# A 3x3 convolution with bfloat16 matmuls: row blocks with a shared middle tap, or every row computed directly

## The chip, the cores and the metric

The kernel runs on one core of a Trainium2 chip. The metric is device time in microseconds (us) of one execution. "PE" is the matrix engine (TensorE), "DVE" the vector engine, "ACT" the scalar engine, "POOL" GpSimd, and "SP" the engine whose queue issues most of the stores.

## The reference

Sixteen images of 64 channels and 64 x 64 pixels are convolved with 128 filters of 3 x 3, with a border of zeros. About nine in ten weights are zero, at random places; neither kernel makes use of that.

```python
batch, c_in, h, w, c_out, k = 16, 64, 64, 64, 128, 3
x_pad = np.pad(x, ((0, 0), (0, 0), (1, 1), (1, 1)))
# for every b, co, ci, kh, kw:
output[b, co] += weight[co, ci, kh, kw] * x_pad[b, ci, kh:kh+h, kw:kw+w]
```

Inputs and output are float32. The input has 16.8 MB, the output 33.6 MB.

## The kernel before

**Placing.** Two images form a pair: the 64 channels of one lie on partitions 0 to 63, those of the other on partitions 64 to 127. There are eight pairs (`NP`), each a resident bfloat16 tile `xs[p]`. Line 63 loads the weights through SP's queue, line 64 the first 9 rows of pair 0 as float32 (`x_head`) through ACT's queue; ACT casts them on line 79. The other rows of pair 0 come in two transfers (lines 65 and 66, up to row 25 and from row 26), and pairs 1 to 7 in one each (line 70). All of these are issued by POOL's queue and cast on the way. While loads are under way, PE runs seven matmuls on zeros (line 77).

**Weights.** DVE casts the weights into `w_bf` (line 101), one group for each kernel row: G0, G1 and G2. `transposed` (lines 91 to 96) turns a group with three matmuls against an identity and copies the result to `wT`. `tap` gives the 64 x 128 weights of a kernel row and column for the upper or lower half of the partitions.

**A product.** `product` (lines 119 to 140) takes two PSUM tiles, one for each image of the pair, and adds up terms. A term is a source, a weight group, a first row and a step between rows. Each term costs three matmuls (kernel columns) for each image, issued in turns: image 0 on the upper 64 rows of the array, image 1 on the lower 64. One matmul covers 8 rows of 64 pixels, 512 columns; at the left and right border 8 x 63, and where a kernel row falls off the image 7 rows.

**Two ways to get 16 output rows.** `direct` (lines 142 to 147) computes 8 rows from three terms, 9 matmuls for each image, and ACT copies one image from PSUM to the output tile `o`, DVE the other. `twos` (lines 149 to 168) computes 16 rows at once. With rows x[r] and x[r+1] of a two-row step, the outputs are

- even row r: G1 (x[r] + x[r+1]) + (G2 - G1) x[r+1] + G0 x[r-1]
- odd row r+1: G1 (x[r] + x[r+1]) + (G0 - G1) x[r] + G2 x[r+2]

so the product of G1 with the sum serves both. POOL adds the row couples into `s` (line 152), PE multiplies by G1 (3 matmuls for each image, 8 rows of sums), ACT copies the result to `pc` (line 159), PE does the even rows and then the odd rows with two terms each (6 matmuls for each image), and DVE adds `pc` to each (line 166). That is 15 matmuls for each image and 16 rows, where `direct` needs 18. The differences G21 = G2 - G1 and G01 = G0 - G1 are made on line 110 by DVE and turned by `transposed`; `differences` is called after the first `direct` group of pair 0.

**Order.** The schedule is written by hand: each engine works in program order. Pairs follow each other, and in a pair four blocks of 16 rows. `BLOCKS` says which blocks are done directly (D): the first of pair 0 and the last of pair 7; the other 30 are T. Output tiles rotate through 7 buffers, PSUM tiles through 8, `s` through 3, `pc` through 4. The stores of a pair, 2 MB for each image, are issued by SP when the pair is done (line 195). Those of pair 7 go out in pieces: rows 0 to 31 and 32 to 47 (line 192, SP), and the last two groups of 8 rows each by themselves (line 183 on SP, line 186 on ACT's queue).

Of the kernel before, what the change touches and what calls it, by code (L numbers as in the profile page):

```python
# [7 lines left out]

FP32 = mybir.dt.float32
BF16 = mybir.dt.bfloat16  # L10
ADD = mybir.AluOpType.add
SUB = mybir.AluOpType.subtract

BLOCKS = {p: "TTTT" for p in range(8)}
BLOCKS[0] = "DTTT"  # L20
BLOCKS[7] = "TTTD"


G0, G1, G2, G21, G01 = range(5)
KW_ORDER = (1, 0, 2)


@with_exitstack
def kernel(
    ctx: ExitStack,  # L30
    tc: tile.TileContext,
    x: bass.AP,
    weight: bass.AP,
    out: bass.AP,
):
    nc = tc.nc

    B, C_IN, H, W = x.shape
    C_OUT, _, KH, KW = weight.shape
    assert (B, C_IN, H, W) == (16, 64, 64, 64) and (C_OUT, KH, KW) == (128, 3, 3)  # L40
    NP = B // 2
    HEAD = 9
    CUT = 26

    const_pool = ctx.enter_context(tc.tile_pool(name="const", bufs=1))
    x_pool = ctx.enter_context(tc.tile_pool(name="x", bufs=1))
    s_pool = ctx.enter_context(tc.tile_pool(name="s", bufs=3))
    p_pool = ctx.enter_context(tc.tile_pool(name="pc", bufs=4))
    o_pool = ctx.enter_context(tc.tile_pool(name="o", bufs=7))
    psum_pool = ctx.enter_context(  # L50
        tc.tile_pool(name="psum", bufs=8, space=bass.MemoryType.PSUM)
    )

    ctx.enter_context(tc.manual_schedule())


    def pair(p):
        return x[2 * p : 2 * p + 2].rearrange("n i h w -> (n i) h w")

    xs = [x_pool.tile([128, H, W], BF16, name=f"x{p}") for p in range(NP)]  # L60
    w_sb = const_pool.tile([C_OUT, C_IN * KH * KW], FP32, name="w_sb")
    x_head = const_pool.tile([128, HEAD, W], FP32, name="x_head")
    nc.sync.dma_start(out=w_sb, in_=weight.rearrange("o i kh kw -> o (i kh kw)"))
    nc.scalar.dma_start(out=x_head, in_=pair(0)[:, 0:HEAD, :])
    nc.gpsimd.dma_start(out=xs[0][:, HEAD:CUT, :], in_=pair(0)[:, HEAD:CUT, :])  # L65
    nc.gpsimd.dma_start(out=xs[0][:, CUT:H, :], in_=pair(0)[:, CUT:H, :])  # L66
    ident = const_pool.tile([128, 128], BF16, name="ident")
    make_identity(nc, ident)
    for p in range(1, NP):
        nc.gpsimd.dma_start(out=xs[p], in_=pair(p))  # L70


    idle_rhs = const_pool.tile([128, 512], BF16, name="idle_rhs")
    nc.vector.memset(idle_rhs, 0.0)  # L74
    idle_ps = psum_pool.tile([128, 512], FP32, name="ps")
    for _ in range(7):
        nc.tensor.matmul(idle_ps, idle_rhs[:, 0:128], idle_rhs, start=True, stop=True)  # L77

    nc.scalar.copy(out=xs[0][:, 0:HEAD, :], in_=x_head)  # L79

    w_v = w_sb.rearrange("o (i k) -> o k i", k=KH * KW)
    w_bf = const_pool.tile([C_OUT, 5, 4 * C_IN], BF16, name="w_bf")
    w_bf4 = w_bf.rearrange("o g (k i) -> o g k i", k=4)
    wT = const_pool.tile([128, 5, 3, C_OUT], BF16, name="wT")

    def tap(g, kw, n):
        return wT[64 * n : 64 * n + 64, g, (kw - n) % 3, :]

    def transposed(g, copy):
        wps = psum_pool.tile([128, 4, 128], FP32, name="ps")
        for j in range(3):
            src = w_bf[:, g, C_IN * j : C_IN * (j + 2)]
            nc.tensor.matmul(wps[:, j, :], src, ident, start=True, stop=True)  # L95
        copy(out=wT[:, g], in_=wps[:, 0:3, :])  # L96

    for g in (G1, G0, G2):
        for a, b in ((0, 3), (3, 4)):
            k = 3 * g + a % 3  # L100
            nc.vector.tensor_copy(out=w_bf4[:, g, a:b, :], in_=w_v[:, k : k + b - a, :])  # L101
    transposed(G1, nc.scalar.copy)
    transposed(G0, nc.vector.tensor_copy)
    transposed(G2, nc.scalar.copy)

    def differences():
        for g, m in ((G21, 2), (G01, 0)):
            for a, b in ((0, 3), (3, 4)):
                k, k1 = 3 * m + a % 3, 3 + a % 3
                nc.vector.tensor_tensor(  # L110
                    out=w_bf4[:, g, a:b, :],
                    in0=w_v[:, k : k + b - a, :],
                    in1=w_v[:, k1 : k1 + b - a, :],
                    op=SUB,
                )
            transposed(g, nc.scalar.copy)


    def product(terms, rows):


        ps = [psum_pool.tile([128, rows, W], FP32, name="ps") for _ in range(2)]
        todo = [(t, kw) for t in terms for kw in KW_ORDER]
        for i, ((src, g, first, step), kw) in enumerate(todo):
            n_src = src.shape[1]
            lo = 0 if first >= 0 else 1
            hi = rows if first + (rows - 1) * step < n_src else rows - 1
            c_lo, c_hi = max(0, 1 - kw), min(W, W + 1 - kw)
            a = first + lo * step
            b = first + (hi - 1) * step + 1  # L130
            for n in range(2):
                q = slice(64 * n, 64 * n + 64)
                nc.tensor.matmul(  # L133
                    ps[n][:, lo:hi, c_lo:c_hi],
                    tap(g, kw, n),
                    src[q, a:b:step, c_lo + kw - 1 : c_hi + kw - 1],
                    start=(i == 0),
                    stop=(i == len(todo) - 1),
                )
        return ps  # L140

    def direct(p, o, r0, rows):
        ps = product(
            [(xs[p], G1, r0, 1), (xs[p], G0, r0 - 1, 1), (xs[p], G2, r0 + 1, 1)], rows
        )
        nc.scalar.copy(out=o[0][:, r0 : r0 + rows, :], in_=ps[0])  # L146
        nc.vector.tensor_copy(out=o[1][:, r0 : r0 + rows, :], in_=ps[1])  # L147

    def twos(p, o, r0):
        t0 = r0 // 2  # L150
        s = s_pool.tile([128, 8, W], BF16, name="s")
        nc.gpsimd.tensor_tensor(  # L152
            out=s, in0=xs[p][:, r0 : r0 + 16 : 2, :], in1=xs[p][:, r0 + 1 : r0 + 16 : 2, :], op=ADD
        )
        shared = product([(s, G1, 0, 1)], 8)
        pc = []
        for n in range(2):
            c = p_pool.tile([128, 8, W], FP32, name="pc")
            nc.scalar.copy(out=c, in_=shared[n])  # L159
            pc.append(c)  # L160
        even = [(xs[p], G21, r0 + 1, 2), (xs[p], G0, r0 - 1, 2)]
        odd = [(xs[p], G01, r0, 2), (xs[p], G2, r0 + 2, 2)]
        for first, terms in ((r0, even), (r0 + 1, odd)):
            ps = product(terms, 8)
            for n in range(2):
                nc.vector.tensor_tensor(  # L166
                    out=o[n][:, first : r0 + 16 : 2, :], in0=ps[n], in1=pc[n], op=ADD
                )

    for p in range(NP):  # L170
        o = [o_pool.tile([C_OUT, H, W], FP32, name="o") for _ in range(2)]
        last = p == NP - 1
        for blk in range(4):
            r0 = 16 * blk
            if BLOCKS[p][blk] == "T":
                twos(p, o, r0)
            else:
                for r, rows in ((r0, 8), (r0 + 8, 8)):
                    direct(p, o, r, rows)
                    if p == 0 and blk == 0 and r == r0:  # L180
                        differences()
                    if last and blk == 3:
                        nc.sync.dma_start(
                            out=out[2 * p][:, r : r + rows, :], in_=o[0][:, r : r + rows, :]
                        )
                        nc.scalar.dma_start(
                            out=out[2 * p + 1][:, r : r + rows, :], in_=o[1][:, r : r + rows, :]
                        )
            if last and blk in (1, 2):
                a, b = (0, 32) if blk == 1 else (32, 48)  # L190
                for n in range(2):
                    nc.sync.dma_start(out=out[2 * p + n][:, a:b, :], in_=o[n][:, a:b, :])
        if not last:
            for n in range(2):
                nc.sync.dma_start(out=out[2 * p + n], in_=o[n])
# [30 lines left out]
```

## Time and profile before

| | |
|---|---|
| time, median of 3 runs | 132.43 us (130.78 to 132.56) |
| time of the profiled execution | 132.56 us |
| its span, first to last instruction | 130.8 us |
| matmuls on line 133 | 972: 792 from `x`, 180 from `s` |
| DVE additions on line 166 | 120, 686 ns each, 75.3 us |
| DVE subtractions on line 110 | 4, 944 ns mean, 3.5 us |
| POOL additions on line 152 | 30, 1164 ns each, 34.8 us |
| ACT copies on line 159 | 60, 589 ns each, 32.2 us |
| ACT copies on line 146, DVE copies on line 147 | 4 and 4, 586 and 692 ns |
| HBM traffic | 17.07 MB read, 33.55 MB written |

The page of a profile shows the busy time of each engine, the span in 40 slices (a digit is the busy share in tenths, "PEclk" the granted clock of PE), and the chain of work that ended last. A timeline lists instructions in order of time as start, duration, engine, line and operation; "SPq" is the issuing queue of SP. A stretch lists, after its length, the busy time and number of instructions of PE, weight load, DVE, ACT and POOL, then the granted clock, the share of the DMA engines and GB/s.

### The profile page before, as it was taken

Reading aid. Unit: us, or ns where it says so; the run is one execution under the profiler, and the core shown is the slowest. Engines: PE = TensorE matmul, PEld = TensorE weight load, DVE = VectorE, ACT = ScalarE, POOL = GpSimd, SP = SyncE. Lnnn points to the kernel's source line nnn. Section 1 sums busy time; section 2 is a strip of 40 time slices with the busy share of each in tenths; the row PEclk is TensorE's granted clock in tenths of the full one; section 3 lists DMA queues with packets and bytes.
Section 4 is the critical chain, followed back from the end, with each engine's and each line's share of the span. In section 5 each row is a group of like instructions: output and inputs, shape, how many; then the busy total and the mean of one; then the engine's idle time right before and its main releaser. Section 6 shows DMA issues by size and latency. Waiting matters only on the chain.

```text
span 130.8 us, 2474 instructions
## 1 busy us (share of the span) xinstructions
PE 113.5 (87%) x994; PEld 49.5 (38%) x994; DVE 84.0 (64%) x136; ACT 38.4 (29%) x70; POOL 40.5 (31%) x45
## 2 busy tenths in 40 slices
PE   6692699999999999999999999999999999994000
PEld 2140234444444444444444444444444444441000
DVE  0418424778777877787778777777777777783000
ACT  3311213333333333333333333333333333302000
POOL 6818203333333333333333333324333300000000
PEclk9999559999999999999999999999999999999655
DMA  4999999999999999999999999999599929989991
GB/s 85 246 201 215 215 210 220 215 213 195 288 328 316 316 328 316 368 446 431 416 448 411 431 441 401 451 426 411 238 406 401 401 85 401 481 376 418 392 385 39
DMA packets 4764, 42.55 MB, mean 325 GB/s; under 512 B 528, under 2 KB 528, under 8 KB 1808
## 3 DMA queue, kind: packets, MB, share of 16 engines
q1 hardware_dynamic: 3024, 33.33, 61.1%
q0 software_dynamic: 1296, 8.24, 31.0%
q10 hardware_dynamic: 432, 0.82, 1.8%
q8 instruction: 8, 0.13, 0.4%
q14 instruction: 4, 0.03, 0.1%
HBM read 17.07 MB, written 33.55 MB: 387 GB/s over the span
## 4 chain that ended last, share of the span: by engine, by line
PE 84%; DVE 4%; DMA 3%; issue 0%
PE ps L133 82%; DMA w_sb<-in_weight_dram 3%; DVE w_bf L110 3%; PE ps L95 2%; DVE o L147 1%; DVE w_bf L101 0%
## 5 line engine op out<-in xcount | busy, mean ns | idle before, releaser
L133 PE MATMUL ps<-x,wT 64*128 64x504 bf16 (+3 forms) x792 | 92.7, 383 | 0.0
L166 DVE TENSOR_TENSOR o<-ps,pc 128x512 f32<-128x512 f32 x120 | 75.3, 686 | 22.3 <-PE ps L133 20.0
L133 PEld LDWEIGHTS <-wT 64*128 64x128 bf16 x972 | 47.5, 96 | 59.7 <-issue 4.8
L152 POOL TENSOR_TENSOR s<-x 128x512 bf16<-128x512 bf16 x30 | 34.8, 1164 | 61.9 <-PE ps L133 47.6
L159 ACT COPY pc<-ps 128x512 f32<-128x512 f32 x60 | 32.2, 589 | 62.4 <-issue 59.6
L133 PE MATMUL ps<-s,wT 64*128 64x512 bf16 (+1 forms) x180 | 24.9, 384 | 0.0
L147 DVE COPY o<-ps 128x512 f32<-128x512 f32 x4 | 2.8, 692 | 9.1 <-PE ps L133 9.1
L95 PE MATMUL ps<-ident,w_bf 128*128 128x128 bf16 x15 | 2.6, 290 | 4.7 <-DVE w_bf L110 3.5
L146 ACT COPY o<-ps 128x512 f32<-128x512 f32 x4 | 2.3, 586 | 10.9 <-PE ps L133 10.9
L77 PE MATMUL ps<-idle_rhs 128*128 128x512 bf16 x7 | 3.2, 630 | 1.2 <-DVE idle_rhs L74 1.2
L101 DVE CAST w_bf<-w_sb 128x192 bf16<-128x192 f32 (+1 forms) x6 | 1.7, 390 | 3.8 <-DMA w_sb<-in_weight_dram 3.8
L70 POOL DMA_DIRECT2D x<-in_x_dram x7 | 3.7, 553 | 1.2 <-DMA x<-in_x_dram 1.2
L95 PEld LDWEIGHTS <-w_bf 128*128 128x128 bf16 x15 | 1.2, 107 | 7.1 <-DVE w_bf L110 4.4
L110 DVE TENSOR_TENSOR w_bf<-w_sb 128x192 bf16<-128x192 f32 (+1 forms) x4 | 3.5, 944 | 0.0
L96 ACT CAST wT<-ps 128x384 bf16<-128x384 f32 x4 | 1.9, 479 | 4.4 <-PE ps L95 4.4
L77 PEld LDWEIGHTS <-idle_rhs 128*128 128x128 bf16 x7 | 0.9, 139 | 2.6 <-issue 1.4
L79 ACT ACT_TABLE_LOAD x1 | 1.3, 1283 | 1.2 <-PEq L210 1.2
L79 ACT CAST x<-x_head 128x576 bf16<-128x576 f32 x1 | 0.7, 671 | 2.7 <-DMA x_head<-in_x_dram 2.7
L65 POOL DMA_DIRECT2D x<-in_x_dram x1 | 0.7, 693 | 0.8 <-POOLq L210 0.8
L74 DVE MEMSET idle_rhs<- 128x256 uint32 x1 | 0.3, 272 | 0.9 <-PEq L210 0.9
L96 DVE CAST wT<-ps 128x384 bf16<-128x384 f32 x1 | 0.6, 558 | 0.0
L66 POOL DMA_DIRECT2D x<-in_x_dram x1 | 0.5, 536 | 0.0
(6 smaller groups left out, 0.9 us busy)
## 6 DMA issues: line engine op xcount, KB each, us to landing
out_dram<-o SPq DMA_DIRECT2D x14, 2048.0 KB, 14.1
x<-in_x_dram POOLq DMA_DIRECT2D x7, 1024.0 KB, 25.2
out_dram<-o SPq DMA_DIRECT2D x2, 1024.0 KB, 9.4
out_dram<-o SPq DMA_DIRECT2D x2, 512.0 KB, 10.9
x<-in_x_dram POOLq DMA_DIRECT2D x1, 608.0 KB, 8.3
out_dram<-o ACTq DMA_DIRECT2D x2, 256.0 KB, 8.5
out_dram<-o SPq DMA_DIRECT2D x2, 256.0 KB, 10.4
x_head<-in_x_dram ACTq DMA_DIRECT2D x1, 288.0 KB, 4.4
```

Of the source, the lines that this page charges most:

```text
L70: nc.gpsimd.dma_start(out=xs[p], in_=pair(p))
L77: nc.tensor.matmul(idle_ps, idle_rhs[:, 0:128], idle_rhs, start=True, stop=True)
L79: nc.scalar.copy(out=xs[0][:, 0:HEAD, :], in_=x_head)
L95: nc.tensor.matmul(wps[:, j, :], src, ident, start=True, stop=True)
L96: copy(out=wT[:, g], in_=wps[:, 0:3, :])
L110: nc.vector.tensor_tensor(out=w_bf4[:, g, a:b, :], in0=w_v[:, k : k + b - a, :], in1=w_v[:, k1 : k1 + b - a, :], op=SUB,)
L133: nc.tensor.matmul(ps[n][:, lo:hi, c_lo:c_hi], tap(g, kw, n), src[q, a:b:step, c_lo + kw - 1 : c_hi + kw - 1], start=(i == 0), stop=(i == ...
L146: nc.scalar.copy(out=o[0][:, r0 : r0 + rows, :], in_=ps[0])
L147: nc.vector.tensor_copy(out=o[1][:, r0 : r0 + rows, :], in_=ps[1])
L152: nc.gpsimd.tensor_tensor(out=s, in0=xs[p][:, r0 : r0 + 16 : 2, :], in1=xs[p][:, r0 + 1 : r0 + 16 : 2, :], op=ADD)
L159: nc.scalar.copy(out=c, in_=shared[n])
L166: nc.vector.tensor_tensor(out=o[n][:, first : r0 + 16 : 2, :], in0=ps[n], in1=pc[n], op=ADD)
```

## The change

`twos`, `differences`, the table `BLOCKS`, the pools of `s` and `pc` and the two weight groups G21 and G01 go. All 64 groups of 8 rows of a pair's two images are computed by `direct`. Loads, first casts, matmuls on zeros, the casts and transposes of G0, G1 and G2, and the stores with their order stay. The core of the diff:

```diff
-BLOCKS = {p: "TTTT" for p in range(8)}
-BLOCKS[0] = "DTTT"
-BLOCKS[7] = "TTTD"
-G0, G1, G2, G21, G01 = range(5)
+G0, G1, G2 = range(3)
...
-    s_pool = ctx.enter_context(tc.tile_pool(name="s", bufs=3))
-    p_pool = ctx.enter_context(tc.tile_pool(name="pc", bufs=4))
...
-    def differences():
-        for g, m in ((G21, 2), (G01, 0)):
-            for a, b in ((0, 3), (3, 4)):
...
-            transposed(g, nc.scalar.copy)
...
-    def twos(p, o, r0):
...
         for blk in range(4):
             r0 = 16 * blk
-            if BLOCKS[p][blk] == "T":
-                twos(p, o, r0)
-            else:
-                for r, rows in ((r0, 8), (r0 + 8, 8)):
-                    direct(p, o, r, rows)
-                    if p == 0 and blk == 0 and r == r0:
-                        differences()
...
+            for r in (r0, r0 + 8):
+                direct(p, o, r, 8)
+                if last and blk == 3:
+                    nc.sync.dma_start(out=out[2 * p][:, r : r + 8, :], in_=o[0][:, r : r + 8, :])
+                    nc.scalar.dma_start(
+                        out=out[2 * p + 1][:, r : r + 8, :], in_=o[1][:, r : r + 8, :]
+                    )
```

More of the change, by code (lines that the diff above doesn't have):

```diff
@@ L10 @@
 BF16 = mybir.dt.bfloat16
-ADD = mybir.AluOpType.add
-SUB = mybir.AluOpType.subtract
-BLOCKS = {p: "TTTT" for p in range(8)}
-BLOCKS[0] = "DTTT"
-BLOCKS[7] = "TTTD"
-G0, G1, G2, G21, G01 = range(5)
+G0, G1, G2 = range(3)
 KW_ORDER = (1, 0, 2)
@@ L83 @@
     w_v = w_sb.rearrange("o (i k) -> o k i", k=KH * KW)
-    w_bf = const_pool.tile([C_OUT, 5, 4 * C_IN], BF16, name="w_bf")
+    w_bf = const_pool.tile([C_OUT, 3, 4 * C_IN], BF16, name="w_bf")
     w_bf4 = w_bf.rearrange("o g (k i) -> o g k i", k=4)
-    wT = const_pool.tile([128, 5, 3, C_OUT], BF16, name="wT")
+    wT = const_pool.tile([128, 3, 3, C_OUT], BF16, name="wT")
     def tap(g, kw, n):
@@ L104 @@
     transposed(G2, nc.scalar.copy)
-    def differences():
-        for g, m in ((G21, 2), (G01, 0)):
-            for a, b in ((0, 3), (3, 4)):
[L109 to L115, printed above, removed]
-            transposed(g, nc.scalar.copy)
     def product(terms, rows):
@@ L147, in direct @@
         nc.vector.tensor_copy(out=o[1][:, r0 : r0 + rows, :], in_=ps[1])
-    def twos(p, o, r0):
[L150 to L168, printed above, removed]
     for p in range(NP):
@@ L174 @@
             r0 = 16 * blk
-            if BLOCKS[p][blk] == "T":
-                twos(p, o, r0)
-            else:
-                for r, rows in ((r0, 8), (r0 + 8, 8)):
-                    direct(p, o, r, rows)
-                    if p == 0 and blk == 0 and r == r0:
-                        differences()
[L182 to L188, printed above, removed]
+            for r in (r0, r0 + 8):
[5 more added lines that the diff above has]
+                    )
             if last and blk in (1, 2):
```

## The prediction

> **What bounds the kernel now.** I read the page's slices first (which engine has no holes), then the chain of work that ended last, then the timelines of its two ends, then the stretches of the store drain. The slices:
>
> ```profile
> span 130.8 us, 2474 instructions
> ...
> PE 113.5 (87%) x994; PEld 49.5 (38%) x994; DVE 84.0 (64%) x136; ACT 38.4 (29%) x70; POOL 40.5 (31%) x45
> ...
> PE   6692699999999999999999999999999999994000
> ...
> PEclk9999559999999999999999999999999999999655
> DMA  4999999999999999999999999999599929989991
> ```
>
> Two rows have no holes: PE from slice 6 to 36, and the DMA engines nearly from 2 us to the end. The chain tells which of them carries:
>
> ```profile
> 7.06 3.27 PE ps L133 x18
> ...
> 10.35 0.69 DVE o L147
> 11.04 3.29 DVE w_bf L110 x3
> ...
> 14.38 0.50 PE ps L95 x3
> 14.88 104.48 PE ps L133 x954
> ```
>
> From 14.88 us on it is PE's convolution matmuls without a break for 104.48 us; no wait of PE on a DMA is listed. Ahead of that lies a hole in which PE waits for the weight differences (line 110). The timeline of PE prices the hole:
>
> ```profile
> 6.99 3.29 PE L133 MATMUL ps<-x,wT 64*128 64x512 bf16 x18
> 11.87 0.28 PE L95 MATMUL ps<-ident,w_bf 128*128 128x128 bf16 x2 [1.59 <-DVE w_bf L110]
> ...
> 14.81 4.02 PE L133 MATMUL ps<-x,wT 64*128 64x512 bf16 x18
> 18.62 1.40 PE L133 MATMUL ps<-s,wT 64*128 64x512 bf16 x6
> 19.86 2.76 PE L133 MATMUL ps<-x,wT 64*128 64x512 bf16 x24
> ```
>
> A row's end is modelled: the next matmul starts 0.17 us before it (19.86 + 2.76 = 22.62, next start 22.45). So the first group of 18 ends its stream at 10.28 - 0.17 = 10.11, and PE could have gone on there, but does at 14.81. From there to 19.86 it is at half clock (2 us stretches show a granted 0.75, 0.50, 0.50, 0.55 from 12 to 20 us, then 1.00). The first group was cold too, although its slices show 9: the zero matmuls before it start 0.43 us apart.
>
> Now the pace, and the end, from the timeline of the last 30 us:
>
> ```profile
> 105.70 0.81 PE L133 MATMUL ps<-s,wT 64*128 64x512 bf16 x6
> ...
> 106.66 0.93 SPq L195 DMA_DIRECT2D out_dram<-o  x2
> ...
> 108.86 0.81 PE L133 MATMUL ps<-s,wT 64*128 64x512 bf16 x6
> ...
> 112.10 0.81 PE L133 MATMUL ps<-s,wT 64*128 64x512 bf16 x6
> 112.75 6.57 PE L133 MATMUL ps<-x,wT 64*128 64x512 bf16 x60
> ```
>
> The two images' matmuls start together, so I count couples. An inner block of 16 rows is 15 couples, 108.86 to 112.10: 3.24/15 = 0.216 us each. A block at an image's edge takes 108.86 - 105.70 = 3.16; three of its couples have 7 rows instead of 8, so these take (3.16 - 12 x 0.216)/3 = 0.189. Steps of 1 or 2 in the rows read cost the same: the 30 couples from 112.75, 18 of them of the plain form, take 6.57 - 0.17 = 6.40, or 0.213, three of them short ones.
>
> The end is not PE's. Stretches of 1 us:
>
> ```profile
> 106.00:107.00 1.00, 1.00 (x14) 0.40 (x12) 1.00 (x3) 0.41 (x1) 0.00 (x0) 1.00 0.00 0
> 107.00:108.00 1.00, 1.00 (x14) 0.48 (x12) 0.42 (x2) 0.66 (x2) 0.00 (x0) 1.00 0.62 262
> ...
> 127.00:128.00 1.00, 0.00 (x0) 0.00 (x0) 0.00 (x0) 0.00 (x0) 0.00 (x0) 0.50 0.78 289
> ```
>
> The last two columns are DMA share and GB/s. The queue is empty at 106.66, when pair 6's stores are issued; then 8.39 MB (pairs 6 and 7) flow without a hole from about 107.4 to 127.8, 411 GB/s, long after PE's last matmul at 119.3. So the end hangs on T6, the issue of pair 6's stores: T6 + 21.1 is the last byte, T6 + 24.1 the span's end.
>
> **The change part by part, against the profiled execution (span 130.8, time 132.56; the median of the runs is 132.43, so 0.1 below).**
>
> 1. *Matmuls.* 30 blocks of 15 couples become 18 each. A direct group (8 rows, 9 couples) takes 9 x 0.216 = 1.94 us, one at an edge 6 x 0.216 + 3 x 0.189 = 1.86; an image pair 6 x 1.94 + 2 x 1.86 = 15.39, against some 12.8 now. All of it is on the path.
> 2. *Differences.* Four subtractions (944 ns mean), six transposes and two ACT casts go, and with them the hole from 10.11 to 14.81, 4.7 us. What comes next are groups 2 to 4 of pair 0; are they late? Rows 9 to 25 land at 1.24 + 5.9 = 7.1, the rest at 1.93 + 8.3 = 10.2, pair 1 from 3.0 + 12.1 = 15.1; needed at 10.1, 14.0 (rows above 25) and 23.6. None is.
> 3. *Clock.* The half clock between 13 and 20 us followed the hole. Twelve couples took 19.86 - 14.81 = 5.05 instead of 2.59: 2.5 us gained if PE stays busy, which it does. The first group I leave at its 3.12, and bound it: 1.86 when warm (1.3 less); cold for as much longer as the half-clock spell's half, 3.4 us, costs half of that, 1.7 more.
> 4. *POOL's 30 additions (34.8 us), ACT's 60 partial copies (32.2), DVE's 120 additions (75.3)* go. They lie beside PE, which never waited for them after 14.9: nothing gained. In their place 64 ACT copies (586 ns) and 64 DVE copies (692 ns), one of each per 1.94 us group: hidden behind PE, with 8 PSUM buffers, four groups, between. Uncovered, only the last copy shows: stream end to store issue is 0.20 (10.11 to 10.31) + 0.59 + 0.03 = 0.82, as against 0.96 now (105.70 to 106.66).
> 5. *Queues.* No DMA is added, dropped or moved: 7 + 2 loads on POOL, 20 stores on SP, two on ACT. SP's stores now wait on ACT and DVE copies instead of DVE additions; behind each waiting store there are only later stores. First stores go out at 23.6 + 0.8 = 24.5 instead of 29.9, into the loads. Seven output buffers: pair 3's second tile (needed at 23.64 + 2 x 15.39 + 1.9 = 56.3) reuses pair 0's first. Were the stores to wait for all loads (8.2 MB at 213 GB/s from 2 us: 41 us) and then take 4.2 MB at 411, they would end at 51. Hidden even so.
>
> *Sum.* Pair 0 ends at 10.11 + 6 x 1.94 + 1.86 = 23.64, pair 6 at 23.64 + 6 x 15.39 = 115.98. T6 = 115.98 + 0.82 = 116.8, that is 10.1 later (81 more couples at 0.216 = 17.5, less 4.7, less 2.5, less 0.1 and rounding). Pair 7 ends at 131.4, its last store is issued at 132.2; the DMA engines, busy with 411 GB/s from 117.5, come to these last 0.5 MB at 136.7, so the drain still sets the end: 116.8 + 24.1 = 140.9. With the 1.8 us between span and time: **142.7 us**.
>
> Two rules of the Trainium skill, each beside its row. The trace moved 17.07 + 33.55 MB of HBM traffic in 130.8 us, 387 GB/s. "DMA: Bandwidth & Descriptors" (Specifications) gives a limit of about 358 GB/s per core; by it both kernels would need 141 us, and the change would cost nothing. The trace already exceeds that limit, so the sum leaves it out. On the clock, the half-speed spell after the hole agrees with "TensorE: Matmul & The Clock Gate" (Part 1), by which an idle window of some 3.4 us halves it; the page adds that the window runs free of the kernel, so that the warm-up point differs from run to run. By that, one window more or less at half speed is 1.7 us, near the 1.8 between the lowest and highest time of before; no trace here shows a second phase.
>
> **Rivals.**
> - *The DMA engines are the bound, and the added matmuls hide (the other side).* For: their row is nearly full from 2 us. Then filling today's holes (92 to 96 and 104 to 107.4, some 4.7 us by share) ends the span at 126.1: 127.9 us, faster. It decides if T6 stays at 106.66: 495 couples between 10.11 and 105.84, 0.193 us each. Against: 0.214 is the mean in three separate rows above, and PE waits for no DMA.
> - *The drain is faster, PE sets the end.* The last store is issued at 132.2. A 2 MB store took 6.4 us at best, 5.1 of them transfer: 1.3 fixed, plus 1.3 for the last 0.5 MB: 135, about 137 us in time. The drain must hold 524 GB/s, seen in single microseconds only; the best long stretch (slices of 401 to 451) gives 431, 0.9 us less than forecast.
> - *A cold start:* no clock gain until a window later, 144.4; with a slow drain too (385 GB/s, the last full slice, +1.4), 145.8.
> - *The change does less than it says:* resident inputs, uncast first rows and matmuls on zeros stand in both kernels; only the shared middle tap goes. That is what is priced.
>
> **How the numbers follow.** Forecast 0.80 (own range 141.2 to 144.1: warm start 1.3 lower, clock and drain up to 1.4 higher); cold start or slow drain 0.11 (144.4 to 145.8); faster drain 0.06 (137 to 140.5); DMA bound 0.03 (127.9). Warm start plus best drain is 142.7 - 1.3 - 0.9 = 140.5; the range 140.3 to 145.3 leaves out the last two cases and little more. Two per cent, 2.6 us, is about what a measurement tells from no change: faster 0.02, same 0.01, slower 0.97.
>
> **What would show it.** Right: PE unbroken from 7.0 to 131.5 us, no half clock between 10 and 130, couples at 0.216, pair 6's stores issued near 116.8 with an empty queue before, last bytes near 138. Wrong: a different couple pace (step 1), a hole near 10 or 56 us (steps 2, 5), a half-clock spell (step 3), waits of PE on ACT or DVE (step 4), or a queue that drains before the last store.

## The result, and the profile after

| | before | after |
|---|---|---|
| time, median of 4 runs | 132.5 us (130.78 to 132.87) | 141.5 us (140.85 to 142.61) |
| ratio | | 1.0735, 95% interval 1.0591 to 1.0879 |
| span of the profiled execution | 130.8 us | 140.4 us |
| its own time | 132.56 us | 142.15 us |

The forecast was 142.7 us, with a span of 140.9. The chain of work that ended last in the changed kernel (start, length, what):

```profile
6.85 124.39 PE ps L108 x1152
...
131.26 0.69 DVE o L122
```

The hole is gone: from 6.85 us to 131.24 us PE works on the convolution. Its timeline shows how the start runs through, with no entry between the first group and the rest:

```profile
5.29 1.56 PE L82 MATMUL ps<-ident,w_bf 128*128 128x128 bf16 x9 [0.93 <-DVE w_bf L88]
6.78 17.45 PE L108 MATMUL ps<-x,wT 64*128 64x512 bf16 x152
```

From the timeline of the end, all engines:

```profile
116.44 0.81 SPq L142 DMA_DIRECT2D out_dram<-o  x2
...
131.99 0.34 ACTq L133 DMA_DIRECT2D out_dram<-o  x1
```

Pair 6's stores (T6) go out at 116.44, and the last store at 131.99. The stretches of 1 us show what the DMA engines do from there (last two columns: share and GB/s):

```profile
116.00:117.00 1.00, 1.00 (x14) 0.48 (x10) 0.56 (x1) 0.42 (x1) 0.00 (x0) 1.00 0.00 0
117.00:118.00 1.00, 1.00 (x14) 0.45 (x10) 0.21 (x1) 0.26 (x1) 0.00 (x0) 1.00 1.17 492
...
137.00:138.00 1.00, 0.00 (x0) 0.00 (x0) 0.00 (x0) 0.00 (x0) 0.00 (x0) 0.50 0.54 199
```

An empty queue, then some 20.5 us of unbroken stores until 137.5, and the span ends at 140.4 = T6 + 24.0. In the kernel before it was T6 + 24.1. The page's slices show no half-clock spell before PE's work is done, and that the DMA engines, nearly without a hole before, now have some in the second half:

```profile
PEclk9999999999999999999999999999999999999975
DMA  4999999999999999999999954993099707999992
```

### The profile page after: what moved, and what is told of

It is laid out like the page before. It is cut to its first block, busy times and chain, and to the rows that moved or that the text cites. A ratio compares the mean times of both kernels' runs of the same rounds, so it can differ in the third digit from the quotient of the medians.

```text
span 140.4 us, 2591 instructions
## 1 busy us (share of the span) xinstructions
PE 129.0 (92%) x1168; PEld 57.1 (41%) x1168; DVE 46.7 (33%) x72; ACT 40.4 (29%) x68; POOL 5.6 (4%) x15
## 4 chain that ended last, share of the span: by engine, by line
PE 90%; DMA 3%; DVE 1%; issue 0%
PE ps L108 89%; DMA w_sb<-in_weight_dram 3%; PE ps L82 1%; DVE o L122 0%; DVE w_bf L88 0%
## 5 line engine op out<-in xcount | busy, mean ns | idle before, releaser
L108 PE MATMUL ps<-x,wT 64*128 64x504 bf16 (+3 forms) x1152 | 124.4, 377 | 0.0
L108 PEld LDWEIGHTS <-wT 64*128 64x128 bf16 x1152 | 55.5, 95 | 68.7 <-issue 1.5
L122 DVE COPY o<-ps 128x512 f32<-128x512 f32 x64 | 44.3, 692 | 80.8 <-PE ps L108 80.8
L121 ACT COPY o<-ps 128x512 f32<-128x512 f32 x64 | 37.5, 586 | 86.9 <-PE ps L108 86.9
L82 PE MATMUL ps<-ident,w_bf 128*128 128x128 bf16 x9 | 1.5, 306 | 1.0 <-DVE w_bf L88 0.9
L82 PEld LDWEIGHTS <-w_bf 128*128 128x128 bf16 x9 | 0.7, 112 | 2.4 <-DVE w_bf L88 2.4
L83 ACT CAST wT<-ps 128x384 bf16<-128x384 f32 x2 | 1.0, 479 | 0.8 <-PE ps L82 0.8
```

The lines of the kernel that those rows point to most:

```text
L108: nc.tensor.matmul(ps[n][:, lo:hi, c_lo:c_hi], tap(g, kw, n), src[q, a:b:step, c_lo + kw - 1 : c_hi + kw - 1], start=(i == 0), stop=(i == ...
```

## Experiments

Every ratio is to the kernel before, run on the same chip; its median was 130.9 to 131.3 us there. The experiments ran on three chips; times from different chips are compared by these ratios. Theory A is the prediction's: PE's stream sets T6, and the drain from T6 sets the end. The main rival, B, is that the DMA engines set the time and PE's work hides behind them.

### The hole put back into the changed kernel

```diff
                 direct(p, o, r, 8)
+                if p == 0 and r == 0:
+                    differences()
```

with the two weight groups G21 and G01 allocated again; nothing reads them.

> The changed kernel (span 140.4 us) with the differences put back after the first group, though nothing uses them: the hole of PE alone. Theory of the prediction (the hole and the half clock after it lie wholly on the path): PE pauses from 9.7 to about 14.6 (4.9 us), then 12 couples at half clock (2.5 us); pair 6's stores go out 7.4 us later, at about 123.8, and the span is 147.8, time 149.5 us. Rival (the start is hidden behind the DMA engines, which are busy then with loads): time unchanged, 141 to 142.6 us.

Measured: 144.25 us (143.21 to 145.83), ratio 1.0964 (1.0892 to 1.1036), against 1.0735 and, on a third chip, 1.0843 (1.0769 to 1.0917) for the changed kernel. By the ratios the hole costs 1.6 to 3.0 us, not 7.4. The intervals touch, so the times alone do not settle whether it is hidden; the trace does. It is of the longest execution (145.83 us), whose clock was at half from 7.5 to 14.4 us. Pair 6's stores go out at 119.96, 3.5 later than in the changed kernel: 2.4 for the hole, 1.1 for the half clock behind it, and the span, 144.0, is again T6 + 24.0. So rival B is wrong here. PE's timeline says why the hole is short:

```profile
11.11 1.09 PE L83 MATMUL ps<-ident,w_bf 128*128 128x128 bf16 x6 [1.22 <-DVE w_bf L99]
12.13 1.46 PE L122 MATMUL ps<-x,wT 64*128 64x512 bf16 x6
```

The second group starts at 12.13, not near 14.6. DVE's four subtractions took 1.26 us in place of 3.54. What is missing beside them is POOL: in the kernel before its first three additions of row couples ran at 10.30 to 13.96, over the subtractions at 10.96 to 14.50; this kernel has no additions. From the timelines of POOL and DVE in the kernel before, and of DVE in this one:

```profile
10.30 3.66 POOL L152 TENSOR_TENSOR s<-x 128x512 bf16<-128x512 bf16 x3 [2.34 <-DMA x<-in_x_dram]
10.96 3.54 DVE L110 TENSOR_TENSOR w_bf<-w_sb 128x192 bf16<-128x192 f32 x4
...
10.56 1.26 DVE L99 TENSOR_TENSOR w_bf<-w_sb 128x192 bf16<-128x192 f32 x4
```

That made a new theory: POOL and DVE hold each other up.

### The same, with POOL's first three additions

```diff
+    for r in (16, 32, 48):
+        s = s_pool.tile([128, 8, W], BF16, name="s")
+        nc.gpsimd.tensor_tensor(
+            out=s, in0=xs[0][:, r : r + 16 : 2, :], in1=xs[0][:, r + 1 : r + 16 : 2, :], op=ADD
+        )
     for p in range(NP):
```

> The changed kernel with the differences put back (as in the run before, where the four subtractions took 1.0 us and the hole of PE 2.4), and with POOL's first three additions of row couples put back beside them; nothing uses either. Theory formed from that run (POOL's additions and DVE's subtractions hold each other up): the subtractions take about 2.5 to 3.5 us again, the hole grows to 4 to 5 us, the time is 1.5 to 2.5 us above the run without the additions. Rival (the short subtractions had another cause, such as the DMA traffic or chance): 1.0 us of subtractions, a hole of 2.4, time as without the additions.

Measured: 148.1 us (147.56 to 149.47), ratio 1.1298 (1.1203 to 1.1393): by the ratios 4.4 us more than without the additions. From the timelines of POOL and DVE in this kernel:

```profile
9.40 3.66 POOL L142 TENSOR_TENSOR s<-x 128x512 bf16<-128x512 bf16 x3 [2.21 <-DMA x<-in_x_dram]
9.58 4.02 DVE L101 TENSOR_TENSOR w_bf<-w_sb 128x192 bf16<-128x192 f32 x4
```

and PE's:

```profile
10.96 0.28 PE L85 MATMUL ps<-ident,w_bf 128*128 128x128 bf16 x2 [2.06 <-DVE w_bf L101]
12.11 0.29 PE L85 MATMUL ps<-ident,w_bf 128*128 128x128 bf16 x1 [0.86 <-DVE w_bf L101]
13.48 0.50 PE L85 MATMUL ps<-ident,w_bf 128*128 128x128 bf16 x3 [1.09 <-DVE w_bf L101]
13.91 1.46 PE L124 MATMUL ps<-x,wT 64*128 64x512 bf16 x6
```

The subtractions take 4.02 us again, in the same three steps as in the kernel before. The theory holds; the cost was larger than expected, 4.4 us instead of 1.5 to 2.5. The hole itself, 5.2 us from 8.7 to 13.9 against 2.4 us without the additions, explains 2.8 of it, and the two profiled spans, 146.7 and 144.0, differ by 2.7. The rest goes with the clock, whose mean was 0.957 to 0.966 in these four runs, but 0.976 to 0.986 in three of the four without additions (0.953 in the profiled one); that is argued from the means, not traced. The Trainium skill ("SBUF — State Buffer", Who interferes with whom) states the cause: a DVE instruction with two inputs in SBUF contends with a GpSimd instruction that reads SBUF. The runs agree with it, and with the number of additions that the subtractions meet: 1.26 us beside none, 2.11 beside one (the kernel before without the hole, below), 2.53 beside two (the hole filled with matmuls, below), 3.54 and 4.02 beside three. They also show which engine waits more. In these traces each subtraction that met an addition ended 0.13 to 0.37 us after that addition's end, and the three additions together took 3.66 us beside subtractions, 3.36 where the subtractions had run earlier.

### The hole filled with matmuls on zeros

```diff
         for j in range(3):
+            for _ in range(zeros[j]):
+                nc.tensor.matmul(zps, idle_rhs[:, 0:128], idle_rhs, start=True, stop=True)
...
-            transposed(g, nc.scalar.copy)
+            transposed(g, nc.scalar.copy, zeros={G21: (7, 0, 4), G01: (5, 0, 0)}[g])
```

in the kernel before; the subtractions and transposes stay where they are.

> The kernel before with its hole left as long as it is, but filled with 16 matmuls on zeros. Theory of the prediction (the half clock is a price of its own, 2.5 us): no half clock between 10 and 120 us, pair 6's stores 2.4 us earlier (104.3), span 128.4, time 130.1 us. Rival (the clock falls in any case, or the hole is the whole loss): span 130.8, time 132.5 us.

Measured: 129.8 us (129.52 to 130.03), ratio 0.9888 (0.9863 to 0.9914). The spell, the stretch at half clock, is gone: in the trace the granted clock rises at 10.1 us and stays until PE's work ends. (This is the first change of the clock that the trace records. Before it the stretches read 1.00, though the zero matmuls at the start follow each other 0.43 us apart.) PE's timeline:

```profile
13.11 1.24 PE L97 MATMUL ps<-idle_rhs 128*128 128x512 bf16 x5
...
14.45 2.12 PE L137 MATMUL ps<-x,wT 64*128 64x512 bf16 x18
16.40 0.81 PE L137 MATMUL ps<-s,wT 64*128 64x512 bf16 x6
17.05 2.76 PE L137 MATMUL ps<-x,wT 64*128 64x512 bf16 x24
```

A group of 18 takes 1.95 us (14.45 to 16.40), where it took 3.81 (14.81 to 18.62), and the twelve couples behind the hole take 2.60 (14.45 to 17.05) in place of 5.05. So the half clock is a price of its own, 2.45 us in the traces; the rival is wrong. The hole did not quite keep its length: POOL's additions began at 9.21, only two of them met the subtractions, and the hole was 4.15 us (10.30 to 14.45) instead of 4.70. The profiled spans differ by 3.0 (127.8 and 130.8, on two chips), but the medians on one chip by 1.5 only, where 2.4 were forecast. Why it is less there stays open: the mean clock of the seven executions of before on this chip, 0.939 to 0.941, is that of the profiled one (0.941), so a spell of another length is not what the record suggests.

### The kernel before without the hole

```diff
-BLOCKS[0] = "DTTT"
+BLOCKS[0] = "DDTT"
...
+                    if p == 0 and r == 24:
+                        transposed(G21, nc.scalar.copy)
+                        transposed(G01, nc.scalar.copy)
```

The transposes are taken out of `differences` in return.

> The kernel before with the second block of pair 0 direct too (3 couples more) and the transposes of the differences after it, so that PE has other work while the vector engine subtracts. Theory of the prediction for the matmul side: hole (4.7) and half clock (2.5) go, 3 couples (0.65) and about 0.9 of transposes come; pair 6's stores go out at about 101.1, 5.6 earlier. If the drain from that moment set the end alone, the span would be 125.2. Theory with the DMA engines as the next bound: their work has holes of only 4.7 us in the kernel before, so the span stops at 126.1, time 127.9 us, and the queue is never empty before pair 6's stores. Rival (the hole was hidden): 132.5 us.

Measured: 128.0 us (127.41 to 128.36), ratio 0.9745 (0.9707 to 0.9784). The profiled span is 126.3. T6 is 100.48, and T6 + 24.1 would be 124.6. Against the profile of before, on another chip, PE gained 6.2 us, and the end only 4.5: here the DMA engines are the limit, as the theory said, which had the span stop at 126.1. The page's slices, to be set beside the same row of before:

```profile
DMA  4999999999999999999999999999999999999980
```

### Only the subtractions moved

The four subtractions run right after the casts of the weights, at 6.7 us, before POOL has additions; their transposes stay behind the first direct group.

```diff
+    differences()
+
     for p in range(NP):
...
                     if p == 0 and blk == 0 and r == r0:
-                        differences()
+                        transposed(G21, nc.scalar.copy)
+                        transposed(G01, nc.scalar.copy)
```

> The kernel before with the four subtractions moved ahead, to where DVE is free at 7.2 us and POOL has no additions yet; their transposes stay behind the first direct group. Theory (contention with POOL made them long): they take about 1.0 to 1.3 us, the hole shrinks to 0.5 us of transposes, no half clock; pair 6's stores go out near 100.0, a microsecond earlier than in the kernel with two direct blocks at the start. Theory of the DMA engines as the next bound: the end does not follow that microsecond; span about 126.3, time about 3 per cent under before, as there. Rival (the end hangs on pair 6's stores alone): span 124.1, 1.7 per cent less than there.

Measured: 127.9 us (127.43 to 128.02), ratio 0.9735 (0.9658 to 0.9813), with the kernel above (0.9745) the fastest of this study that compute the whole result. The four subtractions take 1.27 us. T6 is 99.99, and T6 + 24.1 = 124.1, but the span is 126.2. That T6 is half a microsecond earlier than in the kernel above does not show in the end (126.2 against 126.3).

### The transfers by themselves

```diff
-            [(xs[p], G1, r0, 1), (xs[p], G0, r0 - 1, 1), (xs[p], G2, r0 + 1, 1)], rows
+            [(xs[p], G1, r0, 1)], rows
```

The changed kernel without the terms of the upper and lower kernel row; loads, copies and stores are all there.

> The changed kernel without the terms of the upper and lower kernel row: 24 of 72 couples for an image pair, all loads, copies and stores kept. PE then needs 41 us. Theory that the DMA engines are the next bound: loads and stores back to back take 118 to 121 us from 2 us on, span 123 to 126.5, time 125 to 128 us. If the DMA engines were far from a bound: below 110 us.

Measured: 126.9 us (two runs, 126.66 and 127.10), span 124.9. The slices of its page:

```profile
PE   6699793794790592992100698199095000000000
...
DMA  3999999999999999999999999999999999999992
```

PE has two thirds less to do, and the DMA engines' row is as full as in the two kernels above: some 125 us of span is what the loads and stores need. On this chip the kernel before (131.2 us) stands 4.3 us above that, the one with early subtractions 1.0, and the changed kernel (142.3) 15.4.

### Where the matmuls begin to count

The kernel with early subtractions, with 3 and with 12 more of its blocks direct:

```diff
 BLOCKS[7] = "TTTD"
+for p in (1, 3, 5):
+    BLOCKS[p] = "TTDT"
```

```diff
 BLOCKS[7] = "TTTD"
+for p in (1, 2, 3, 4, 5, 6):
+    BLOCKS[p] = "DTDT"
```

> The kernel before with early subtractions (span 126.2, pair 6's stores at 100.0) and 3 more of its 30 shared blocks done directly, one each in pairs 1, 3 and 5. Theory (the span is the larger of the transfers' own 126.2 and the store of pair 6 plus 24.1): 9 couples more put the stores at 101.9, which gives 126.0, so the time stays at about 128 us. Rival (matmuls are on the path throughout): 1.9 us more, 129.9 us.

Measured: 127.8 us (127.42 to 128.09), ratio 0.9761 (0.9719 to 0.9804); T6 at 102.08, span 126.3:

```profile
102.08 0.93 SPq L198 DMA_DIRECT2D out_dram<-o  x2
```

Three direct blocks cost nothing that shows.

> The same with 12 more blocks direct, two each in pairs 1 to 6. Theory: 36 couples more put pair 6's stores at 107.8, which is past the point where the transfers hide it, so span 131.9, time 133.7 us, half of the direct form's loss paid in full from the point on. Rival (each block costs the same from the start): 100.0 + 7.8 counted from 126.2, 134.0 span, 135.8 us. Rival (all of it hidden): 128 us.

Measured: 133.3 us (132.19 to 134.35), ratio 1.0153 (1.0090 to 1.0216). The profiled execution is the longest (134.35 us); its T6 is 108.48, its span 132.4 = T6 + 23.9:

```profile
108.48 0.89 SPq L198 DMA_DIRECT2D out_dram<-o  x2
```

The time is near that of the theory (133.7); the two rivals, 135.8 and 128, are off by 2.5 and 5.3. So in these kernels the direct form's cost is a ramp with a flat foot: nothing while T6 + 24 lies below the transfers' 126.2, and above it one for one, as far as the two points there show (this kernel's T6 and the changed one's are 8.0 us apart, their spans 8.0).

### The drain

```diff
+            if p == NP - 2 and blk in (1, 3):
+                a = 0 if blk == 1 else 32
+                for n in range(2):
+                    nc.sync.dma_start(out=out[2 * p + n][:, a : a + 32, :], in_=o[n][:, a : a + 32, :])
-        if not last:
+        if p < NP - 2:
```

> The changed kernel with pair 6 stored in two halves of 32 rows, each issued when it is done; matmuls untouched. Theory of the prediction (the end is the drain of 8.39 MB that starts at pair 6's stores): the first half (2.1 MB) goes out 7.7 us earlier into an empty queue, the drain ends about 2.5 us earlier, span about 137.8, time 139.5 us. Rival (the end follows PE's last matmul and copy by a fixed latency): span 140.4, time 142 us as before.

Measured: 138.9 us (137.82 to 139.50), ratio 1.0573 (1.0521 to 1.0625), against 1.0735 and 1.0843 of the changed kernel on other chips. The stretches of this kernel:

```profile
121.00:122.00 1.00, 1.00 (x12) 0.49 (x10) 0.28 (x1) 0.14 (x1) 0.00 (x0) 1.00 0.22 90
122.00:123.00 1.00, 1.00 (x14) 0.44 (x10) 0.47 (x1) 0.51 (x1) 0.00 (x0) 1.00 0.08 25
123.00:124.00 1.00, 1.00 (x12) 0.43 (x10) 0.22 (x1) 0.08 (x1) 0.00 (x0) 1.00 0.18 74
124.00:125.00 1.00, 1.00 (x12) 0.49 (x10) 0.53 (x1) 0.56 (x1) 0.00 (x0) 1.00 1.07 442
```

The queue is nearly empty once more before pair 7's first half (25 to 90 GB/s), so the backlog that set the end is shorter; the span is 136.0, 4.4 less than in the changed kernel's trace, of which 1.0 is an earlier start of the full clock (last copies at 130.19 against 131.23); 2.6 was expected of the rest, 3.4 came. The end was indeed the drain, and not a fixed latency behind PE.

### Both copies on DVE

```diff
-        nc.scalar.copy(out=o[0][:, r0 : r0 + rows, :], in_=ps[0])
+        nc.vector.tensor_copy(out=o[0][:, r0 : r0 + rows, :], in_=ps[0])
```

> The changed kernel with both copies of a group on DVE instead of one on ACT: 128 copies of 0.69 us, 88.6 us of DVE's time, 1.38 us in each group of 1.94 us. Theory of the prediction (copies are hidden behind PE; only the last ones show): stores go out 0.6 us later, time 142.5 to 143 us, not to be told from the changed kernel. Rival (emptying PSUM limits the pace): PE pauses between groups, pace above 1.94 us, time above 145 us.

Measured: 142.9 us (141.32 to 144.11), ratio 1.0875 (1.0795 to 1.0956), not to be told from the 1.0843 of the changed kernel on another chip. Twice the copies on one engine, and PE, busy 129.3 us, does not wait for them:

```profile
L108 PE MATMUL ps<-x,wT 64*128 64x504 bf16 (+3 forms) x1152 | 124.7, 377 | 0.0
...
L121 DVE COPY o<-ps 128x512 f32<-128x512 f32 x64 | 44.3, 692 | 43.4 <-PE ps L108 43.4
```

The last columns are idle time before the group and its releaser: PE has none, DVE waits 43.4 us for PE.

### The changed kernel once more

> The changed kernel once more, unchanged, on the same chip as the others of this call. Theory that the moment at which PE's clock rises differs from run to run (9.6, 8.9, 4.1, 10.1, 9.3 and 4.8 us in six traces with the same first instructions): a clock that rises once somewhere between 4 and 10.5 us, no half clock after it, times spread over 1.5 us or so around 141.5. Rival (the moment is set by the kernel's first instructions): 8.9 us again and a spread below 0.5 us.

Measured: 142.3 us (141.94 to 142.82), ratio 1.0843 (1.0769 to 1.0917). In this trace the granted clock rises at 10.4 us, in the first one it rose at 8.9. The spread was 0.9 us, less than expected. The theory of a moment that differs from run to run holds: in all traces of the study it lies between 4.0 and 10.5 us, and on one of the chips alone between 4.1 and 10.1.

## Why the prediction was right

The forecast of 142.7 us was 0.6 above the profiled execution and 1.2 above the median. Step by step:

1. *Matmuls: right.* The first stores of the 14 whole ones go out at 24.04 and those of pair 6 at 116.44: 92.4 us for six pairs, 15.40 each; forecast 15.39.
2. *Differences: right in the sum, wrong in what is behind it.* The hole of 4.7 us went, and nothing was late next; no wait of PE stands after 5.3 us. But the hole was not the price of the subtractions. These need 1.26 us by themselves; beside POOL's additions they took 3.54. Since the hole was read from the trace and left whole, the sum did not suffer; as far as the reason goes, that is luck.
3. *Clock: right in the traces, the size open in the times.* No half clock between 10 and 130 us. Taken away alone, the spell gave 2.45 us in the trace, where 2.5 was forecast, but the medians differ by 1.5 only. The start was 0.2 us earlier (first convolution matmul at 6.78, not 6.99) and the clock rose at 8.9, so the first group took 2.9 instead of 3.12: these 0.4 us are what T6 is early (116.44, forecast 116.8).
4. *POOL, ACT and DVE: wrong on POOL, without effect on the sum.* "Nothing gained" from POOL's 30 additions is wrong: three of them stood on the path, through DVE. The other part is shown: the copies are hidden, even when one engine makes all of them.
5. *Queues: right.* No wait for output buffers appears; the span ends at T6 + 24.0, forecast T6 + 24.1.

Of the rivals, the DMA-bound one fell as a forecast, since the changed kernel's DMA engines stand still at times. It was nearer than its chance of 0.03 suggests, though: the transfers alone need a span of 124.9 us, and had the kernel before started 5 us earlier, its PE time would already have been hidden. The kernel before already stood above that bound: on one chip its spans were 128.8 to 130.5, those of the kernel with early subtractions 125.7 to 126.2. In times on that chip, the direct form (142.3 us) stands 14.4 above the kernel with early subtractions (127.9) and 11.1 above the kernel before (131.2), which lost 3.3 us at its start that the change gave back. The drain that the second rival thought faster was not: it took 24.0 us from T6, and the end came forward when half of pair 6's stores was issued two blocks earlier. The cold start did not come about in the profiled execution: the first group took 2.9 us, no longer than in the kernel before.

## What to carry to other kernels

Three things carry over, as far as one kernel can show them. Sum a change up to the moment that starts the last transfers, and add the drain from there; and measure the transfers by themselves once, since here a change of matmul work cost nothing below that floor and its full price above. A stall beside two engines that both read SBUF need not be the price of the waiting work alone: look at what else ran in its window. Removing work can also remove a stall elsewhere, so the reverse experiment, putting only the stall back, tells what the forecast got right by its reasons.

## What the runs showed of the hardware

- DVE's four subtractions with two SBUF inputs took 1.26 us alone, and 2.11, 2.53 and 3.54 to 4.02 us beside one, two and three of POOL's additions. Three additions took 3.36 us alone and 3.66 beside subtractions.
- After the same zero matmuls at the start, the first rise of PE's granted clock that a trace records came at 4.0 to 10.5 us. Half-clock spells before 20 us lasted 3.4 or 6.8 us; two kernels had one from about 7.5 us on, after an early rise at about 4 us, with no hole of PE between but the microsecond after the zero matmuls (4.3 to 5.4) and two of under 0.2 us. The Trainium skill ("TensorE: Matmul & The Clock Gate", Part 1) has a window of about 3.4 us that runs free of the kernel; these lengths and the differing moment agree with it.
- HBM traffic was 361 GB/s over the changed kernel's span, 387 over that of before and 405 with a third of the matmuls. The limit of about 358 GB/s that the prediction weighed ("DMA: Bandwidth & Descriptors" of the Trainium skill, Specifications, which works it out as a stack's 716 GB/s divided by two cores) did not hold for these kernels, which run on one core.
